# A recurrence of sixteen pairs of heads, regrouped: four pairs in lockstep instead of two staggered chains

## The chip, the cores and the metric

The kernel runs on one core of one Trainium2 chip, as one program. The metric is device time in microseconds of one launch; the time of a kernel is the median of its runs. The engines are named as in the profile: PE (matrix multiplication, with PEld its weight loads), DVE (vector), ACT (scalar), POOL (GpSimd), SP (here it issues nearly all DMAs).

## The reference, cut to what matters

A trunk of two layers over 512 tokens of width 2048. Layer 0 is a gated attention and is untouched. Layer 1 is RWKV-7 time mixing with 32 heads of 64:

```python
def step(S, inp):
    r_t, w_t, k_t, v_t, a_t, b_t = inp
    sa = jnp.einsum('bhvk,bhk->bhv', S, a_t)
    S = S * w_t[:, :, None, :] + sa[..., None] * b_t[:, :, None, :] \
        + v_t[..., None] * k_t[:, :, None, :]
    y_t = jnp.einsum('bhvk,bhk->bhv', S, r_t)
    return S, y_t
...
_, y = lax.scan(step, S0, xs)
...
y = (y - mean) * lax.rsqrt(var + LNX_EPS)
y = y * lnx_w.reshape(H, N).astype(f32) + lnx_b.reshape(H, N).astype(f32)
y = y + jnp.sum(rh * kh * r_k.astype(f32), axis=-1, keepdims=True) * vh
...
return (y * jax.nn.silu(z)) @ w_out
```

`r`, `k`, `v` and `z` are four projections of 2048 by 2048 of mixed inputs; decay `w`, `a` and a part of `v` come from small low-rank products.

## The kernel before, in words

Activations lie with features on the 128 partitions and the 512 tokens on the free axis, so a tile of 128 features is a pair of heads: 16 pairs, j = 0 to 15. Each projection is 16 tiles of 16 steps, and a step is three matmuls of 128x128 by 512 columns (`mm3`: high by high, low by high, high by low part of the float32 operands). On PE these are the rows `pj<-hi,whi`, `pj<-hi,wlo`, `pj<-lo,whi`; I call the three a triple. Their weights come by DMA (`raw<-in_wr`, `in_wv`, `in_wz`, `in_wo`), four triples to a load; ACT makes the high part (`whi`), DVE the low one (`wlo`).

**What sets the order.** Every engine issues in the order in which the code was written, and that order comes from a planner, `Flow`: side tasks are generators that yield planned delays, and `backbone` writes the projection triples and lets due tasks put their instructions between them. Its clock advances with the columns of the matmuls written. `HOP` is the planned length of a step of the recurrence. The layer-1 tiles run in the order r, v, z, output.

**The recurrence** is done by chunks of 64 tokens, eight per pair. What a chunk needs is made earlier by `keys` (tensors `atd`, `bkd` in DRAM), by `invert` and `inverse` (`qtd`), by `lora_up` (`ipd`), `recept` (`rTd`) and `values` (`vvd`, and transposed `vtd`), each stored for a pair with `sp.dma_start`.

`stage` (line 1454) loads a pair: `rt`, `bk` in four DMAs, `prk`, and for each half of four chunks `L`, `QP` (two DMAs for each head) and `SV`. Four halves may be staged ahead (`free["half"]`). `stage_half` makes the products of a half: for each chunk and head one `S<-L,bk` matmul of 128 columns, copied by ACT to `L` and `GP`, masked by POOL, then transposes `S<-ident,bk` copied to `tok`. At the end of a pair it makes a bonus term (`bv`, with two means matmuls `S<-mhi`, `S<-mlo`).

`chain` (line 1567) runs a pair's eight chunks, one after the other, in three steps per chunk. In each a few float32 matmuls of 64 columns, for the two heads, go to PE, and DVE takes the result:

- `x<-SV,L` and `y<-L,SV`; DVE copies `x` to `xs`, POOL scales the state for the next chunk (`SV<-SV,dec`);
- `x<-xs,QP`; DVE copies it to `SV`, over the state just read;
- `x<-SV,tok`; DVE adds it to the next chunk's `SV`; `y<-GP,SV` finishes the output. A last chunk has no `x<-SV,tok`.

`hop` waits for the planner's next multiple of `HOP`. Two pairs are active at a time, half a pair apart, so PE gets two pairs' matmuls of a step together. When a pair ends, `chain` normalizes it (`S<-mhi,centerr`, `S<-mhi,blkr`, scale and shift on DVE) and stores `ypd`; `gated` multiplies by the z projection.

SP's queue is one for all of these loads and stores and for the weights. A DMA that waits holds what stands behind it.

Of the kernel before, what the change touches and what calls it, by code (L numbers as in the profile page):

```python
# [17 lines left out]
P = 128  # L18
# [7 lines left out]
NCH = T // C  # L26
LW, LA_, LV = 96, 96, 64
# [102 lines left out]
def body(ctx, tc, a, out, dbg=None, stop=0):  # L130
# [81 lines left out]
    atd = dr.tile([KT, P, NCH, C], F, name="atd")  # L212
    bkd = dr.tile([KT, P, 2, NCH, C], F, name="bkd")
# [4 lines left out]
    ipd = dr.tile([KT, P, T], F, name="ipd")  # L218
    aad = dr.tile([KT, P, T], F, name="aad")
    svd = dr.tile([KT, P, T], F, name="svd")  # L220
    rTd = dr.tile([KT, P, T], F, name="rTd")
    vvd = dr.tile([KT, P, T], F, name="vvd")
    vtd = dr.tile([KT, T, P], F, name="vtd")
    ypd = dr.tile([KT, P, T], F, name="ypd")
# [806 lines left out]


# [22 lines left out]
    free = {"m": NHP, "eI": 1, "eN": 1, "bk": 1, "B": 1, "gab": 12, "qt": 5, "half": 4, "prk": 2, "sv": 1, "vf": 2}  # L1055
# [149 lines left out]
    def lora_up(q, j, n):  # L1205
# [20 lines left out]
        sp.dma_start((ipd, aad, svd)[n][j], t)  # L1226
# [5 lines left out]
    def values(j, o, e):  # L1232
# [16 lines left out]
        sp.dma_start(vvd[j], vv)  # L1249
# [9 lines left out]
        sp.dma_start(vtd[j].rearrange("(i p) c -> p i c", i=4), vt)  # L1259
# [22 lines left out]
    def keys(q, j):  # L1282
        ip = load(q, ipd[j], "ip", bufs=2)
# [42 lines left out]
        sp.dma_start(atd[j], at)  # L1326
        sp.dma_start(bkd[j], bk)
# [122 lines left out]
    QP, GP, staged = [], [], {}  # L1450

    HC = NCH // 2

    def stage(q, j):
        eI = q.tile([P, NCH, C + 1], F, tag="eI", name="eI", bufs=2)
        rt = load(q, rTd[j], "rt", bufs=2)
        bk = q.tile([P, NCH, 2, C], F, tag="bk", name="bk", bufs=2)
        yield 1
        for i in range(2):
            sp.dma_start(bk[0:64, :, i, :], bkd[j][0:64, i])  # L1460
            sp.dma_start(bk[64:128, :, i, :], bkd[j][64:128, 1 - i])
            yield 1
        dec = q.tile([P, NCH], F, tag="dec", name="dec", bufs=3)
        yield from take("prk")
        prk = q.tile([P, NCH, C], F, tag="prk", name="prk", bufs=2)
        sp.dma_start(prk, ipd[j].rearrange("p (c t) -> p c t", c=NCH))
        rv = c3(rt)
        for cc in range(2):
            yield from take("half")
            cs = slice(HC * cc, HC * cc + HC)  # L1470
            L, SV = ([q.tile([P, HC] + w, F, tag=f"{n}{h}", name=f"{n}{h}", bufs=4)
                      for h in range(2)] for n, w in (("L", [2, C]), ("SV", [C])))
            qp, gp = QP[(2 * j + cc) % 4], GP[(2 * j + cc) % 4]
            for h in range(2):
                s, t = HS[h], OS[h]
                sp.dma_start(L[h][s, :, 0, :], atd[j][s, cs])
                for p in range(2):
                    sp.dma_start(qp[h][s, p::2, :],
                                 qtd[j, 64 * p:64 * p + 64,
                                     4 * h + HC // 2 * cc:4 * h + HC // 2 * (cc + 1), :])  # L1480
                yield 0.5
            while j not in vd:
                yield 0.2
            for h in range(2):
                s, t = HS[h], OS[h]
                sp.dma_start(SV[h][t], vtd[j].rearrange("(c t) d -> t c d", c=NCH)[:, cs, s])
                if cc == 0:
                    pool.memset(SV[h][HS[h], 0, :], 0.0)
            fl.start(fl.t, stage_half(q, j, cc, L, SV, qp, gp, bk, eI, rv, dec, prk))
            yield 3  # L1490

    def stage_half(q, j, cc, L, SV, qp, gp, bk, eI, rv, dec, prk):
        cs = slice(HC * cc, HC * cc + HC)
        yield STW if j else 12
        if cc == 0:
            pool.memset(eI[:, :, 0:1], 1.0)
            act.activation(eI[:, :, 1:], prk, AF.Exp, scale=-EDEC)
            yield 2
            pool.tensor_copy(dec, eI[:, :, C])
        for h in range(2):  # L1500
            s = HS[h]
            dve.tensor_tensor(out=L[h][s, :, 1, :], in0=rv[s, cs], in1=eI[s, cs, 1:],
                              op=OP.mult)
            yield 0.6
            dve.scalar_tensor_tensor(out=prk[s, cs], in0=L[h][s, :, 1, :],
                                     scalar=vecs[s, V_RK, j:j + 1],
                                     in1=bk[s, cs, 1 - h, :], op0=OP.mult, op1=OP.mult)
            yield 0.6
        yield 0.7
        ns = yield from need2("S")  # L1510
        gs = [bank("S") for _ in ns]
        for c in range(HC):
            for h in range(2):
                s = HS[h]
                pe.matmul(gs[h][:, c * P:(c + 1) * P],
                          bk[s, HC * cc + c].rearrange("p a t -> p (a t)"),
                          L[h][s, c].rearrange("p a t -> p (a t)"), start=True, stop=True)
        yield 0.7
        for h in range(2):
            s, t = HS[h], OS[h]  # L1520
            g3 = gs[h].rearrange("p (c n) -> p c n", c=HC)
            act.activation(L[h][t].rearrange("p c a t -> p c (a t)"), g3[t], AF.Copy)
            act.activation(gp[h][s], g3[s, :, C:], AF.Copy)
            read("S", ns[h])
            pool.affine_select(out=L[h][t], in_=L[h][t], pattern=[[0, HC], [1, 2], [1, C]],
                               compare_op=OP.is_ge, fill=0.0, base=-1,
                               channel_multiplier=-1)
            pool.affine_select(out=gp[h][s], in_=gp[h][s], pattern=[[0, HC], [1, C]],
                               compare_op=OP.is_ge, fill=0.0, base=0,
                               channel_multiplier=-1)  # L1530
            yield 0.9
        pool.tensor_tensor(out=bk[:, cs], in0=bk[:, cs],
                           in1=eI[:, cs, C:C + 1].unsqueeze(2).broadcast_to([P, HC, 2, C]),
# [4 lines left out]
        for c in range(HC):  # L1538
            pe.transpose(tr[:, c * P:(c + 1) * P],
                         bk[:, HC * cc + c].rearrange("p a t -> p (a t)"), ident)  # L1540
        yield 0.5
        tok = q.tile([P, HC, 2, C], F, tag="tok", name="tok", bufs=4)
        act.activation(tok.rearrange("p c h t -> p (c h t)"), tr, AF.Copy)
        read("S", n)
        staged[j, cc] = L, SV, qp, gp, dec, tok
        if cc == 0:
            return
        vv = load(q, vvd[j], "vv", bufs=1)
        yield from take("B")
        bo, n = yield from means(q, blkr, prk.rearrange("p c t -> p (c t)"), "mh", "ml")  # L1550
        free["B"] += 1
        yield 0.7
# [5 lines left out]
        staged[j] = bv  # L1558

    active = set()  # L1560
# [6 lines left out]
    def chain(q, j):  # L1567
        active.add(j)
        y = bank("y")
        for c in range(NCH):  # L1570
            last = c == NCH - 1
            i, n = c % HC, (c + 1) % HC
            if i == 0:
                L, SV, qp, gp, dec, tok = staged.pop((j, c // HC))
                nSV = SV
# [254 lines left out]
```

## Time and profile before

| | us |
|---|---|
| median of 3 runs | 2463.61 (2460.46 to 2463.98) |
| the profiled execution's own time | 2465.95 |
| its span, first to last instruction | 2464.2 |
| mean granted clock of PE | 0.983 |
| first and last chain matmul `x<-SV,L` start | 1758.0, 2274.1 |
| last `y<-GP,SV` starts | 2278.6 |
| share of the chain that ended last: PE, of it pj | 72%, 56% |

All operations go through one helper, so every row of the profile has the line L88 (L90 in the changed program) and is told apart by its tiles, written out<-in. Times in windows and timelines are from the span's start. A float32 matmul of 64 columns, and one of 64 rows by 128 columns, leaves two records each: the 256 `x<-SV,L` of the program are 512 in the trace.

### The profile page before, as it was taken

The page shows a single profiled execution, that of the slowest core. Times are in us where ns is not written, and L with a number is a line of the kernel's source. Part 1 is how long each engine was busy: PE and PEld are TensorE (multiplying, and loading weights), DVE is VectorE, ACT ScalarE, POOL GpSimd, SP SyncE. Part 2 cuts the span into 40 slices and gives each one's busy share as a digit, 9 for nine tenths or more (in the row PEclk, how much of TensorE's full clock was granted, in tenths as well). Part 3 has the DMA queues.
Part 4 walks back from the last instruction along what each step waited for, and adds up shares of the span by engine and source line. Part 5 has one row for each costly group of instructions (what it writes and reads, how often), then busy time and mean ns, then how long its engine had stood idle before and what let it go on. Part 6 is the DMA issues. An engine that isn't in the chain of part 4 may idle for free.

```text
span 2464.2 us, 39831 instructions
## 1 busy us (share of the span) xinstructions
PE 2354.1 (96%) x13626; PEld 1811.6 (74%) x13626; DVE 1648.8 (67%) x3130; ACT 1259.0 (51%) x2301; POOL 709.2 (29%) x1154
## 2 busy tenths in 40 slices
PE   6998899999999999998999998989899999999999
PEld 4786677777777778886766776767677677777887
DVE  6977778787887544337796667763467867776322
ACT  3435656555555544226547777743334555555321
POOL 0002424434333100110240239830334444441000
PEclk8999999999999999999999999999899999999999
DMA  8865566666665264445657898867666755554443
GB/s 305 321 221 182 175 198 206 210 206 210 204 213 171 92 227 157 147 137 176 205 168 248 290 287 252 278 208 203 180 169 171 193 161 160 161 161 149 148 146 95
DMA packets 341563, 480.25 MB, mean 195 GB/s; under 512 B 146544, under 2 KB 156912, under 8 KB 337520
## 3 DMA queue, kind: packets, MB, share of 16 engines
q1 hardware_dynamic: 339696, 475.08, 61.5%
q0 software_dynamic: 1664, 2.63, 0.3%
q8 instruction: 108, 1.77, 0.3%
q14 instruction: 95, 0.78, 0.1%
HBM read 381.63 MB, written 95.95 MB: 194 GB/s over the span
## 4 chain that ended last, share of the span: by engine, by line
PE 72%; DVE 8%; DMA 6%; POOL 6%; ACT 4%; issue 3%; SPq 1%; DVEq 0%; ACTq 0%; POOLq 0%
PE pj L88 56%; PE S L88 6%; PE x L88 4%; POOL lane L88 3%; POOL lt L88 3%; PE tr L88 2%; PE pv L88 2%; DVE wlo L88 2%; DVE m L88 2%; PE ss L88 1%; PE y L88 1%; SPq L88 1%; DMA wm<-in_wmodT 1%; DVE wm L88 1%; ACT whi L88 1%
## 5 line engine op out<-in xcount | busy, mean ns | idle before, releaser
L88 PE MATMUL pj<-hi,whi 128*128 128x512 f32 x2416 | 997.9, 413 | 13.3 <-ACT hi L88 8.2
L88 PE MATMUL pj<-hi,wlo 128*128 128x512 f32 x2416 | 959.8, 397 | 6.1 <-DVE wlo L88 6.1
L88 PE MATMUL pj<-lo,whi 128*128 128x512 f32 x2416 | 960.6, 398 | 0.0
L88 DVE TENSOR_TENSOR wlo<-raw,whi 128x512 fp32r<-128x512 f32 (+2 forms) x628 | 479.7, 771 | 263.9 <-ACT whi L88 250.1
L88 ACT ACTIVATE whi<-raw 128x512 fp32r<-128x512 f32 (+2 forms) x628 | 394.5, 634 | 442.2 <-PE pj L88 246.6
L88 PEld LDWEIGHTS pj<-hi,whi 128*128 128x128 f32 x2416 | 459.7, 190 | 119.8 <-ACT hi L88 9.0
L88 PEld LDWEIGHTS pj<-lo,whi 128*128 128x128 f32 x2416 | 458.6, 190 | 108.2 <-DVE lo L88 0.2
L88 PEld LDWEIGHTS pj<-hi,wlo 128*128 128x128 f32 x2416 | 460.6, 191 | 96.3 <-DVE wlo L88 8.1
L88 POOL TENSOR_SCALAR SV<-SV,dec 64x64 f32<-64x64 f32 x224 | 95.7, 428 | 211.7 <-DVE SV L88 196.6
L88 DVE CUSTOM_DVE_ANT_0 wm<-wm,cb 128x1024 f32<-128x1024 f32 x128 | 156.3, 1221 | 0.3
L88 ACT ACTIVATE pr<-Sm,mx 128x128 f32<-128x128 f32 (+3 forms) x128 | 71.6, 559 | 88.9 <-POOL mx L88 88.8
L88 POOL TENSOR_SCALAR mx<-mx 128x1 f32<-128x1 f32 x128 | 65.7, 513 | 162.5 <-DVE mx L88 115.8
L88 POOL TENSOR_SCALAR pr<-pr,rc 128x128 f32<-128x128 f32 (+3 forms) x128 | 97.1, 758 | 28.8 <-DVE rc L88 20.5
L88 DVE COPY SV<-x 64x64 f32<-64x64 f32 x256 | 56.8, 222 | 63.6 <-PE x L88 56.5
L88 DVE CUSTOM_DVE_ANT_0 Sm<-S,cmask 128x128 f32<-128x128 f32 (+3 forms) x128 | 62.2, 486 | 37.2 <-PE S L88 36.6
L88 POOL TENSOR_TENSOR lt<-lane 128x30 f32<-128x30 f32 (+14 forms) x90 | 62.4, 693 | 55.2 <-DMA lane<-mld 48.3
L88 POOL TENSOR_TENSOR lane<-lane,lt 128x30 f32<-128x30 f32 (+14 forms) x90 | 67.8, 753 | 7.0
L88 DVE TENSOR_TENSOR SV<-SV,x 64x64 f32<-64x64 f32 x224 | 49.0, 219 | 25.1 <-PE x L88 19.4
L88 PE MATMUL S<-k,q 128*128 128x128 f32 (+7 forms) x256 | 62.4, 324 | 1.5 <-DMA k<-krow 1.5
L88 POOL TENSOR_TENSOR acc<-acc,sq 128x512 f32<-128x512 f32 x14 | 18.1, 1296 | 150.7 <-ACT sq L88 128.3
L88 PE MATMUL tr<-ident,pr 128*128 128x128 f32 x320 | 56.7, 275 | 4.5 <-ACT pT L88 1.7
L88 PEld LDWEIGHTS tr<-ident,pr 128*128 128x128 f32 x320 | 41.3, 140 | 25.1 <-ACT pT L88 7.9
(324 smaller groups left out, 3376.4 us busy)
## 6 DMA issues: line engine op xcount, KB each, us to landing
wm<-in_wmodT SPq DMA_DIRECT2D x132, 512.0 KB, 4.2
raw<-in_wz SPq DMA_DIRECT2D x128, 256.0 KB, 3.8
raw<-in_wo SPq DMA_DIRECT2D x128, 256.0 KB, 3.5
raw<-in_wv SPq DMA_DIRECT2D x124, 256.0 KB, 3.6
wm<-in_wmodT SPq DMA_DIRECT2D x30, 1024.0 KB, 6.8
raw<-in_wk SPq DMA_DIRECT2D x96, 256.0 KB, 3.7
raw<-in_wr SPq DMA_DIRECT2D x64, 256.0 KB, 4.9
raw<-in_wq SPq DMA_DIRECT2D x56, 256.0 KB, 3.5
```

The source lines that it names most:

```text
L88: self.last = f(*a, **k)
```

## The change

Pairs are taken in four groups of four (`NJ = 4`), and chunks in units of two (`UC = 2`; `NG = 4` groups, `NU = 4` units). One task, `recur`, runs 32 chunk steps of four pairs each, in place of two staggered `chain`s. A step now has eight matmuls of a kind in a row (four pairs, two heads); the DVE copies and adds of a head cover four pairs, 64x256, and the tok product has an `x` bank of its own. `HOP` goes from 2.0 to 3.9. Each chunk but a group's last has three steps with `x`, so there are 32 x 3 - 4 = 92 steps that have an `x` product.

`stage` loads a unit of two chunks of four pairs: `rt`, four `bk`, `prk`, then for each chunk and head one `L`, one `QP` and one `SV` load; four chunks may be staged ahead. It waits for the vectors of all four pairs. `products` makes one chunk's products, `bonus` and `normed` work on a unit; scale, shift and the bonus factor differ by pair and are now applied in four pieces. `gated` takes one of two tokens for its z tile. The DRAM tensors that staging reads are laid out by group and unit, so that their stores by pair are in pieces of 128 tokens (512 B); `bkd` and `vtd` are stored by two DMAs each, `vtd` in pieces of 64 features (256 B).

The core of the diff:

```diff
-    atd = dr.tile([KT, P, NCH, C], F, name="atd")
-    bkd = dr.tile([KT, P, 2, NCH, C], F, name="bkd")
+    atd = dr.tile([NG, P, NU, NJ, UC * C], F, name="atd")
+    bkd = dr.tile([NG, P, NU, 2, NJ, UC * C], F, name="bkd")
...
-    vtd = dr.tile([KT, T, P], F, name="vtd")
+    vtd = dr.tile([NG, T, 2, NJ, DH], F, name="vtd")
...
-        sp.dma_start(vtd[j].rearrange("(i p) c -> p i c", i=4), vt)
+        for h in range(2):
+            sp.dma_start(vtd[j // NJ].rearrange("(i p) h j d -> h j p i d", i=4)[h, j % NJ],
+                         vt[:, :, DH * h:DH * h + DH])
...
-        sp.dma_start(bkd[j], bk)
+        for i in range(2):
+            sp.dma_start(bkd[j // NJ][:, :, i, j % NJ], u3(bk[:, i].rearrange("p c t -> p (c t)")))
...
+        while any(NJ * g + i not in vd for i in range(NJ)):
+            yield 0.2
+        for c in range(UC):
+            yield from take("chunk")
...
+                sp.dma_start(L[h][s, :, 0, :], atd[g][s, u, :, c * C:c * C + C])
+                dve.tensor_copy(L[h][s, :, 1, :], rt[s, :, c])
+                sp.dma_start(qp[h][s], qtd[NJ * g:NJ * g + NJ, 64 * c:64 * c + 64,
+                                           4 * h + u, :].rearrange("j p t -> p j t"))
+                sp.dma_start(SV[h][t], vtd[g][(UC * u + c) * C:(UC * u + c + 1) * C, h])
...
+    def recur(q):
+        for m in range(NG * NCH):
...
+            for j in range(NJ):
+                for h in range(2):
+                    pe.matmul(x[HS[h], 0, j], L[h][:, j, 0, :], SV[h][:, j, :],
+                              start=True, stop=True, skip_group_check=True)
+            xs = q.tile([P, NJ, C], F, tag="xs", name="xs", bufs=2)
+            dve.tensor_copy(xs, x[:, 0])
...
             for h in range(2):
                 s = HS[h]
+                for j in range(0 if last else NJ):
+                    pool.tensor_scalar(nSV[h][s, j, :], SV[h][s, j, :], dec[s, j, c:c + 1],
                                        1.0, op0=OP.mult, op1=OP.mult)
             yield from hop()
+            for j in range(NJ):
+                for h in range(2):
+                    pe.matmul(x[HS[h], 1, j], qp[h][:, j, :], xs[:, j, :],
+                              start=True, stop=True, skip_group_check=True)
             for h in range(2):
-                dve.tensor_copy(SV[h][HS[h], i, :], x[HS[h], C:2 * C])
+                dve.tensor_copy(SV[h][HS[h]], x[HS[h], 1])
...
-    HOP = 2.0
+    HOP = 3.9
```

How the order moves. First PE, in the middle of the recurrence, before: the second step of a chunk (`x<-xs,QP`) of the two active pairs, among triples of a projection.

```order
L88 MATMUL pj<-hi,wlo 128x512
L88 MATMUL pj<-lo,whi 128x512
L88 MATMUL x<-xs,QP_17032 64x64
L88 MATMUL x<-xs,QP_17033 64x64
L88 MATMUL x<-xs,QP_17024 64x64
L88 MATMUL x<-xs,QP_17025 64x64
L88 MATMUL pj<-hi,whi 128x512
```

The same step in the changed program; each pair of rows is the two heads of one of the four pairs.

```order
L90 MATMUL pj<-lo,whi 128x512
L90 MATMUL x<-xs,QP_17042 64x64
L90 MATMUL x<-xs,QP_17043 64x64
L90 MATMUL x<-xs,QP_17042 64x64
L90 MATMUL x<-xs,QP_17043 64x64
L90 MATMUL x<-xs,QP_17042 64x64
L90 MATMUL x<-xs,QP_17043 64x64
L90 MATMUL x<-xs,QP_17042 64x64
L90 MATMUL x<-xs,QP_17043 64x64
L90 MATMUL pj<-hi,whi 128x512
```

A run of four has become a run of eight, and there are fewer of them; what is written between two triples without a projection matmul in between is one run.

Then SP, at the first staging, while the v projection's weights are loaded, before: the loads of pair 0's halves.

```order
L88 DMA L_17082<-atd 64x4x64
L88 DMA QP_17016<-qtd 64x2x64 x2
L88 DMA raw<-in_wv 128x512
L88 DMA L_17083<-atd 64x4x64
L88 DMA QP_17017<-qtd 64x2x64 x2
L88 DMA SV_17084<-vtd 64x4x64
L88 DMA SV_17085<-vtd 64x4x64
L88 DMA raw<-in_wv 128x512
```

In the changed program, the first chunk's loads, behind the store of pair 3's vectors (`vtd<-vt`).

```order
L90 DMA raw<-in_wv 128x512
L90 DMA vtd<-vt 128x4x64 x2
L90 DMA L_17198<-atd 64x4x64
L90 DMA QP_17034<-qtd 64x4x64
L90 DMA SV_17200<-vtd 64x256
L90 DMA L_17199<-atd 64x4x64
L90 DMA QP_17035<-qtd 64x4x64
L90 DMA SV_17201<-vtd 64x256
L90 DMA raw<-in_wv 128x512
```

The first chunk's six loads stand together, right behind the last store they need; fewer staging loads stand between the first weight loads, as they come later.

More of the change, by code (lines that the diff above doesn't have):

```diff
@@ L1464, in stage @@
         yield from take("prk")
[L1465 to L1473, printed above, removed]
+        prk = q.tile([P, NJ, UC, C], F, tag="prk", name="prk", bufs=2)
@@ L1477, in stage @@
[L1477 to L1488, printed above, removed]
@@ L1604, in chain @@
                 for h in range(2):
                     s = HS[h]
-                    dve.tensor_tensor(out=nSV[h][s, n, :], in0=nSV[h][s, n, :],
-                                      in1=x[s, 2 * C:3 * C], op=OP.add)
-            for h in range(2):
-                pe.matmul(y[HS[h], c * C:(c + 1) * C], SV[h][:, i, :], gp[h][:, i, :],
-                          start=False, stop=True, skip_group_check=True)
-            if i == HC - 1:
-                free["half"] += 1
-            if not last:
-                yield from hop()
@@ L1669, in gated @@
         yield 1
+        free["z"] += 1
         if j < KT - 2:
```

268 lines of the change are left out of this document (143 added, 125 removed).

## The prediction

> **What bounds the kernel now.** First the page's busy shares, then the stretch in which the recurrence runs, by windows (PE, PEld, DVE, ACT and POOL busy, granted clock, DMA share, GB/s).
>
> ```profile
> PE 2354.1 (96%) x13626; PEld 1811.6 (74%) x13626; DVE 1648.8 (67%) x3130; ACT 1259.0 (51%) x2301; POOL 709.2 (29%) x1154
> ```
> ```profile
> 1400.00:1500.00 100.00, 92.54 (x461) 70.83 (x461) 74.23 (x93) 77.02 (x139) 43.08 (x53) 0.99 0.90 289
> 1500.00:1600.00 100.00, 93.24 (x817) 72.15 (x813) 75.78 (x95) 74.23 (x144) 89.90 (x126) 0.98 0.87 268
> 1700.00:1800.00 100.00, 87.16 (x536) 65.70 (x535) 45.20 (x101) 29.28 (x53) 28.27 (x70) 0.93 0.70 186
> 1800.00:1900.00 100.00, 98.58 (x892) 72.17 (x891) 72.56 (x195) 44.30 (x83) 42.68 (x87) 1.00 0.62 171
> 1900.00:2000.00 100.00, 94.58 (x835) 69.23 (x833) 79.46 (x204) 53.77 (x97) 46.87 (x88) 0.98 0.66 181
> 2000.00:2100.00 100.00, 99.41 (x900) 72.76 (x900) 70.72 (x193) 57.63 (x96) 45.66 (x90) 1.00 0.58 158
> 2100.00:2200.00 100.00, 99.44 (x902) 72.40 (x903) 72.04 (x195) 61.14 (x98) 43.31 (x88) 1.00 0.59 162
> 2200.00:2300.00 100.00, 99.12 (x693) 73.11 (x694) 65.85 (x154) 54.59 (x90) 23.77 (x42) 1.00 0.47 151
> ```
>
> From 1800 to 2300 PE idles only 8.9 us (1.4 + 5.4 + 0.6 + 0.6 + 0.9). The recurrence is hidden beside the projections, and what sets the end is PE's own work. So a change counts here if it makes that work shorter or lets PE wait. The one weak place is 1700 to 1800: 12.8 us idle, and a mean clock of 0.93. The waits of PE over the recurrence, and the window around that place, say when:
>
> ```profile
> PE S L88 <- ACT vt L88: 5.9, 1, 5.9
> PE x L88 <- DVE SV L88: 4.5, 13, 0.9
> PE pj L88 <- ACT whi L88: 3.5, 1, 3.5
> ```
> ```profile
> 1723.00:1754.00 31.00, 18.16 (x75) 13.02 (x74) 13.61 (x25) 8.96 (x17) 8.79 (x15) 0.78 0.77 206
> ```
>
> All 12.8 us lie between 1723 and 1754 (31.00 less 18.16), just as staging begins, and the clock there averages 0.78. If it switches between full and half, it was at half for 0.44 of 31 us, 13.6 us, which costs at most another 6.8. The start of the recurrence is thus worth up to 19.6 us. Why ACT was late, from the timelines of ACT and SP:
>
> ```profile
> 1726.22 0.63 ACT L88 ACTIVATE whi<-raw 128x512 fp32r<-128x512 f32 x1 [6.22 <-DMA raw<-in_wv]
> ```
> ```profile
> 1719.41 1.26 SPq L88 DMA_DIRECT2D QP<-qtd  x2
> 1720.72 1.26 SPq L88 DMA_DIRECT2D SV<-vtd  x2
> ```
>
> Staging loads take SP about 0.63 us each, and weight loads (raw) stand behind them in the same queue.
>
> **PE's work: fewer runs.** The matmuls of recurrence and staging are the same in number and shape in both programs. What differs is how they are bunched. On PE they interrupt a stream of projection matmuls, and an interruption costs more than its matmuls. Two interruptions (a matmul of 64 columns leaves two records):
>
> ```profile
> 2039.76 0.40 PE L88 MATMUL pj<-lo,whi 128*128 128x512 f32 x1
> 2040.09 0.45 PE L88 MATMUL x<-xs,QP 128*64 128x64 f32 x8
> 2040.47 0.50 PE L88 MATMUL pj<-hi,whi 128*128 128x512 f32 x1
> 2040.80 0.39 PE L88 MATMUL pj<-hi,wlo 128*128 128x512 f32 x1
> 2041.03 0.39 PE L88 MATMUL pj<-lo,whi 128*128 128x512 f32 x1
> ...
> 2042.43 0.40 PE L88 MATMUL pj<-lo,whi 128*128 128x512 f32 x1
> 2042.76 0.34 PE L88 MATMUL x<-SV,tok 128*64 128x64 f32 x4
> 2042.92 0.29 PE L88 MATMUL y<-GP,SV 128*64 128x64 f32 x4
> 2043.04 0.29 PE L88 MATMUL x<-SV,tok 128*64 128x64 f32 x4
> 2043.15 0.29 PE L88 MATMUL y<-GP,SV 128*64 128x64 f32 x4
> 2043.37 0.50 PE L88 MATMUL pj<-hi,whi 128*128 128x512 f32 x1
> 2043.71 0.39 PE L88 MATMUL pj<-hi,wlo 128*128 128x512 f32 x1
> ```
>
> Undisturbed, pj starts are 0.23 apart (2040.80, 2041.03). Within a run, four records take 0.115 (2042.92 to 2043.15 is eight in 0.23), so 0.029 each. From the last pj before a run to the second pj after it there are two pj steps, 0.47, and the records. The first run: 1.04 - 0.47 - 8 x 0.029 = 0.34 us over. The second, twice as long: 1.28 - 0.47 - 16 x 0.029 = 0.35. So the extra hangs on the run and not on its length. A run of transposes alone, with the median of one such transpose:
>
> ```profile
> 1877.02 0.39 PE L88 MATMUL S<-mlo,centerr 128*128 128x512 f32 x1
> 1877.25 0.60 PE L88 MATMUL S<-ident,bk 128*128 128x128 f32 x4
> 1877.61 0.48 PE L88 MATMUL pj<-hi,whi 128*128 128x512 f32 x1
> 1877.93 0.39 PE L88 MATMUL pj<-hi,wlo 128*128 128x512 f32 x1
> ```
> ```profile
> L88 PE MATMUL S<-ident,bk x128: 270/273/421, 1757.5 to 2239.1; 128*128 128x128 f32 x128
> ```
>
> Four transposes are (0.60 - 0.27) / 3 = 0.11 apart, 0.44 in all; 0.91 - 0.47 - 0.44 leaves nothing. They are free of the extra. The means of 512 columns (S<-mlo) are of pj's kind, and I count them with pj.
>
> Counted in the two orders from the first staging product on, runs that hold chain matmuls or staging products fall from 217 to 102; staging products are part of 32 runs in both. 115 x 0.34 = 39 us less PE work. Bounds: 0 if the extra is not the run's, and 115 x 0.35 = 40.
>
> The Trainium skill, "TensorE: Matmul & The Clock Gate", section "Back-to-back issue gap", gives a steady gap of the columns over 2.4 GHz plus about 2.5 ns, with no term for a change of kind between neighbours; by it alone this term would be 0 and the sum 2455. The rows above disagree with it at both chain runs, so I go by the rows.
>
> **The start.** From the first load of a stage on, SP has 50 other DMAs to issue before its eighth weight load in the old order and 26 in the new, 53 and 36 before the tenth: the first stages are halves of two pairs before, two chunks of four pairs now. 24 fewer at 0.63 us is 15 us of SP's time, more than the 12.8 of PE's idling. Against it, the vectors of pairs 0 to 3 are all needed before the first chunk, and their last store and the first load of it stand close together in the new order; SP waits there with weight loads behind it. Later the new order is the denser one (120 against 100 before the 25th). I take half of the 19.6, -10; the ends are -19.6 (no stall left) and +10 (half as much again as before).
>
> **Other edits.** Rows of the operations that change shape, from the views of their tiles:
>
> ```profile
> L88 DVE COPY SV<-x x256: 205/223/230, 1760.8 to 2276.6; 64x64 f32<-64x64 f32 x128
> L88 DVE TENSOR_TENSOR SV<-SV,x x224: 202/220/227, 1763.0 to 2271.9; 64x64 f32<-64x64 f32 x112
> L88 DVE TENSOR_TENSOR L<-rt,eI x64: 407/422/789, 1730.3 to 2228.1; 64x256 f32<-64x256 f32 x64
> L88 POOL TENSOR_SCALAR SV<-SV,dec x224: 310/319/1996, 1730.0 to 2266.2; 64x64 f32<-64x64 f32 x112
> L88 SPq DMA_DIRECT2D bkd<-bk x16: 320/376/403, 1399.2 to 1594.0; - x16
> ```
>
> DVE's 256 copies and 224 adds of 64 columns become 64 and 56 of 256. No PSUM read of 64x256 is in the trace; from 0.22 (64 columns) to 0.42 (256 columns from SBUF) I take the latter: 256 x 0.223 + 224 x 0.22 = 106 us become 50. Splitting prk and the scale and shift by pair gives some of that back. DVE is 66 to 79% busy and hidden by PE, so 0; without the cover it would still be a gain. POOL keeps its 224 decays, but eight stand in a row, 8 x 0.32 = 2.6 us, ahead of the copy that overwrites what they read. In the order, three to five triples of pj, 2.1 to 3.5 us, and a run of 0.8 lie between: enough, though not by much; 0, bounded by the second rival. DMA issues: 64 fewer for QP, 16 more each for bkd and vtd. Stores of bkd come while DMA is 0.90 and 0.87 busy (1400 to 1600), now in pieces of 512 B: from 0 (PE's waits there are on DVE) to 16 x 0.38 = 6 us if each extra issue delays PE; +2, nearer the hidden end. Table loads fall by three, off the path.
>
> **Sum.** Against the profiled execution's own 2465.95 (span 2464.2): -39 - 10 + 2 = 2419. That execution was 2.3 over the median of the runs shown, 2463.61, so the forecast is 2416.
>
> **Rivals.**
> 1. *One chain, more waits.* Two independent chains become one; 92 steps each wait for DVE. For: PE already waited for DVE SV 13 times, 4.5 us, 0.35 each. Against: in the new order most steps stand three to six triples apart, at least 2.1 us, against two copies of 0.42 and one DVE operation ahead. At 0.35 for each step, 92 x 0.35 = 32: 2448.
> 2. *The stall of the start comes back with every group.* Four groups begin with loads for four pairs; if SP's staging holds weight loads back each time, PE loses 19.6 four times instead of once, +59, and -39 + 2 remain: 2485, slower. It decides where more than about four loads of 0.63 stand per weight load while a weight load lasts PE four triples (2.8 us) with no recurrence beside them. For: the later order is denser. Against: from the second group on each triple has recurrence work beside it, so weight loads are needed more rarely, and only four chunks may be staged ahead.
> 3. *The extra is not the run's.* It moves with the steps' matmuls instead: -10 + 2: 2455. The two run lengths speak against it.
> 4. *Short stores of the vectors.* vtd is written in pieces of 256 B instead of 512. If that doubles a landing of 5.3 us,
>
> ```profile
> vtd<-vt SPq DMA_DIRECT2D x3, 256.0 KB, 5.3
> ```
>
> SP waits 5.3 longer ahead of the first chunk, the gain of the start is gone too: 2465.95 - 39 + 5.3 + 2 - 2.3 = 2432. The Trainium skill, "DMA: Bandwidth & Descriptors", section "Specifications", puts line rate at 512 B and up, with read-modify-write below. No run here shows it yet.
>
> That the bunching does not come about is excluded by the order: eight matmuls of a step stand in a row.
>
> **Chances.** Forecast 0.70, its own range 2396 (all of the start and the 8.9 us of idling won) to 2436 (the start +10). Rival 1: 0.14; 2: 0.07; 3: 0.05; 4: 0.04. The range reaches to rival 1, 2396 to 2450, and leaves out 2, 3 and a tail of the forecast. A measurement of this kernel can tell about 0.2%, 5 us, from no change. Slower takes rival 2 and a little of 1, 0.08; within 0.2% are the edges of 1 and 3, 0.04; faster is the rest, 0.88.
>
> **What would show it.** Right: PE busy from the first product to the end of the recurrence about 39 us shorter at unchanged matmul counts; the extra of 0.34 at runs of 16 and 32 records alike; less idling than 12.8 us where staging starts. Wrong: an extra that grows with the run (3); many short waits on DVE SV or xs in PE's list (1); waits on ACT whi at each group's start and a clock under 1.00 there (2); a late vtd with SP's load of SV behind it (4). I am wrong if PE's work falls and its idling rises by as much.

## The result and the profile after

The changed kernel took 2427.65 us (median of 4 runs, 2426.07 to 2435.13), the kernel before 2463.8 in the same comparison (4 runs, 2460.46 to 2468.75). The ratio is 0.9858, with a 95% interval of 0.9831 to 0.9884: faster by 1.4%. The forecast of 2416 was 11.65 us too low, inside its range. The two profiled executions took 2465.95 and 2426.40.

The busy shares of the changed kernel, from its page. PE has lost 42 us of work at the same 13626 instructions, and DVE 42:

```profile
PE 2312.1 (95%) x13626; PEld 1806.3 (74%) x13626; DVE 1607.0 (66%) x2850; ACT 1254.5 (52%) x2298; POOL 701.4 (29%) x1114
```

To compare equal work I count the triples of projection matmuls, which stand in the same order in both programs; a triple is placed by the start of its `pj<-hi,whi`. Triple 1344 is where the stage of the keys begins, 1600 is behind it, staging begins at about 1728, and the recurrence has ended by 2176. The windows between these triples, first of the kernel before (span of the window, then busy us of PE, PEld, DVE, ACT and POOL, the granted clock, the DMA share, GB/s); the rows are triples 1344 to 1600, 1600 to 2176, and inside the latter 1728 to 1792 and 1792 to 1920:

```profile
1360.20:1604.30 244.10, 226.73 (x1513) 175.12 (x1512) 173.96 (x217) 183.10 (x338) 148.29 (x204) 0.99 0.87 277
1604.30:2293.00 688.70, 659.39 (x5602) 489.22 (x5601) 459.81 (x1155) 340.58 (x593) 247.17 (x480) 0.98 0.62 174
1720.40:1809.30 88.90, 76.06 (x530) 56.04 (x529) 43.24 (x106) 28.16 (x52) 27.77 (x56) 0.92 0.67 179
1809.30:1987.80 178.50, 171.66 (x1531) 125.52 (x1529) 139.87 (x359) 89.45 (x163) 76.24 (x150) 0.99 0.65 177
```

The same work in the changed kernel:

```profile
1351.60:1604.00 252.40, 230.87 (x1513) 177.14 (x1512) 171.67 (x217) 183.10 (x338) 146.28 (x203) 0.97 0.91 268
1604.00:2252.60 648.60, 616.62 (x5602) 485.26 (x5602) 422.01 (x877) 337.12 (x591) 242.00 (x441) 0.98 0.66 185
1718.70:1805.70 87.00, 79.11 (x707) 61.71 (x707) 55.10 (x112) 36.83 (x68) 35.70 (x66) 0.96 0.71 187
1805.70:1987.70 182.00, 167.54 (x1654) 130.91 (x1652) 136.48 (x280) 93.64 (x173) 87.83 (x155) 0.97 0.73 193
```

From triple 1600 to 2176 PE did the same 5602 records in 42.8 us less busy time. Its idle time there went from 29.3 (688.70 less 659.39) to 32.0. The stage of the keys took 8.3 longer; half of that is idling (17.4 to 21.5), and half is the same 1513 records taking 4.1 longer at a granted clock of 0.97 instead of 0.99. Up to triple 1344 the changed kernel was 8.6 ahead (1360.2 less 1351.6), and behind triple 2176 it lost 0.8. In sum: -8.6 + 8.3 - 40.1 + 0.8 = -39.6, the difference of the profiled executions (39.55).

What PE waited for from 1690 to 2290, changed kernel:

```profile
PE S L90 <- ACT vt L90: 6.6, 2, 3.8
PE S L90 <- DVE mlo L90: 4.2, 4, 1.6
PE S L90 <- DVE vf L90: 3.1, 1, 3.1
...
PE x L90 <- DVE xs L90: 1.0, 1, 1.0
```

The chain itself hardly waits. What waits is work on the S banks: staging products, transposes and means that stand in PE's order before the engines ahead of them are done.

### The profile page after: what moved, and what is told of

Its sections match the earlier page's. It is cut to its first block, busy times and chain, and to the rows that moved or that the text cites. A ratio compares the mean times of both kernels' runs of the same rounds, so it can differ in the third digit from the quotient of the medians.

```text
span 2424.7 us, 39355 instructions
## 1 busy us (share of the span) xinstructions
PE 2312.1 (95%) x13626; PEld 1806.3 (74%) x13626; DVE 1607.0 (66%) x2850; ACT 1254.5 (52%) x2298; POOL 701.4 (29%) x1114
## 5 line engine op out<-in xcount | busy, mean ns | idle before, releaser
L90 PE MATMUL pj<-hi,whi 128*128 128x512 f32 x2416 | 986.6, 408 | 11.9 <-ACT hi L90 8.2
L90 DVE TENSOR_TENSOR wlo<-raw,whi 128x512 fp32r<-128x512 f32 (+2 forms) x628 | 474.4, 762 | 281.7 <-ACT whi L90 279.3
L90 POOL TENSOR_SCALAR SV<-SV,dec 64x64 f32<-64x64 f32 x224 | 98.3, 461 | 113.5 <-DVE SV L90 71.5
L90 POOL TENSOR_TENSOR bk<-bk,eI 128x512 f32<-128x512 f32 x32 | 36.4, 1137 | 105.9 <-PE S L90 90.1
L90 DVE SCALAR_TENSOR_TENSOR hp<-pj,gate,hp 128x512 f32<-128x512 f32 x16 | 12.0, 751 | 68.8 <-PE pj L90 68.8
## 6 DMA issues: line engine op xcount, KB each, us to landing
raw<-in_wz SPq DMA_DIRECT2D x128, 256.0 KB, 3.8
raw<-in_wo SPq DMA_DIRECT2D x128, 256.0 KB, 3.5
raw<-in_wv SPq DMA_DIRECT2D x124, 256.0 KB, 3.8
raw<-in_wk SPq DMA_DIRECT2D x96, 256.0 KB, 3.6
raw<-in_wr SPq DMA_DIRECT2D x64, 256.0 KB, 4.6
raw<-in_wq SPq DMA_DIRECT2D x56, 256.0 KB, 3.5
```

The lines of the kernel that those rows point to most:

```text
L90: self.last = f(*a, **k)
```

## The experiments

Twelve further runs were made, one of them the changed kernel again. The theory of the prediction was an extra of 0.34 us for each run of chain matmuls. After comparing the two traces a second one stood beside it: the extra is paid at each change of the tile shape that PE's rows name (`128*128`, `128*64` or `64*128`), about 0.17 each, twice for a plain run. (The shape is the pair that stands in each row ahead of the operands' sizes; 128*128 is the full one.) The rival to both was an extra that goes with the matmuls.

**What the extra belongs to: e1_split.** Each step is broken after two of its four pairs:

```diff
                     pe.matmul(x[HS[h], 0, j], L[h][:, j, 0, :], SV[h][:, j, :],
                               start=True, stop=True, skip_group_check=True)
+                if j == 1:
+                    yield 0.95
```

(and the same in the other two steps)

> The new kernel with each of the three matmul steps of a chunk broken after two of its four pairs, so that projection triples come between the halves. Nothing else is changed. Runs that hold chain matmuls or staging products rise from 102 to 158; changes of the tile shape on PE (128*128 for projections, means and transposes, 128*64 for the chain, 64*128 for the staging products) rise from 230 to 389. Theory of the prediction (0.34 us per run): +56 x 0.345 = +19 us of PE busy time, about 2447. Second theory, formed from the rows of both traces (runs of chain matmuls cost 0.35, runs of staging products alone 0.38, runs with both 0.54, runs of transposes 0): the cost is 0.17 us for each change of tile shape: +159 x 0.172 = +27 us, about 2455, with runs of 0.35 for chain matmuls and about 0.7 where products stand between chain matmuls. Rival (the extra belongs to the steps' matmuls, whose number is unchanged): 0, 2428.

Measured: 2475.35 us, ratio to before 1.0058 (1.0045 to 1.0071), slower than before and above all three forecasts. From triple 1728 to 2176, split kernel first, changed kernel second:

```profile
1725.90:2298.70 572.80, 538.57 (x4625) 405.31 (x4624) 358.16 (x738) 285.75 (x495) 216.86 (x397) 0.98 0.59 166
```
```profile
1718.70:2252.60 533.90, 509.31 (x4626) 399.88 (x4626) 355.40 (x742) 289.83 (x499) 217.01 (x397) 0.98 0.65 179
```

PE's busy time rose by 29.3, nearer to the 27 of the shape than to the 19 of the run; the matmuls are the same, so the rival is out. Between the two theories this sum alone is weak: the later kernels with the matmul order of the changed one are busy for 503.4 (e4) to 516.9 (e10) there, and for 529.5 in e3, where the granted clock is 0.92. The rest of the loss in this stretch, 9.6, is idling, which no theory had named: the later halves come so late that the next step waits for its copy.

```profile
PE x L90 <- DVE xs L90: 14.6, 9, 3.0
```

The rows of single runs tell the two theories apart. In the changed kernel, a chain run with products behind it:

```profile
2009.25 0.40 PE L90 MATMUL pj<-lo,whi 128*128 128x512 f32 x1
2009.58 0.69 PE L90 MATMUL x<-SV,L 128*64 128x64 f32 x16
2010.09 0.64 PE L90 MATMUL y<-L,SV 128*64 128x64 f32 x16
2010.66 1.16 PE L90 MATMUL S<-L,bk 64*128 64x128 f32 x16
2011.75 0.50 PE L90 MATMUL pj<-hi,whi 128*128 128x512 f32 x1
2012.09 0.39 PE L90 MATMUL pj<-hi,wlo 128*128 128x512 f32 x1
```

In the split kernel, with the products between the halves of a step:

```profile
2026.71 0.40 PE L90 MATMUL pj<-lo,whi 128*128 128x512 f32 x1
2027.04 0.45 PE L90 MATMUL x<-SV,tok 128*64 128x64 f32 x8
2027.42 1.16 PE L90 MATMUL S<-L,bk 64*128 64x128 f32 x16
2028.51 0.45 PE L90 MATMUL x<-SV,tok 128*64 128x64 f32 x8
2028.80 0.64 PE L90 MATMUL y<-GP,SV 128*64 128x64 f32 x16
2029.36 0.50 PE L90 MATMUL pj<-hi,whi 128*128 128x512 f32 x1
2029.70 0.39 PE L90 MATMUL pj<-hi,wlo 128*128 128x512 f32 x1
```

Both are one run of 48 records of the same kinds, 32 chain and 16 products. From the last pj ahead to the second pj behind, the first takes 2.84 and has three changes of shape; the second takes 2.99 and has four. One change more costs 0.15, in one and the same run.

What a change does stands in the rows of PEld, PE's weight loads. Of the first run, the loads at its first and its last change:

```profile
2009.58 0.55 PEld L90 LDWEIGHTS x<-SV,L 128*64 128x64 f32 x16 [0.36 <-issue]
...
2011.75 0.19 PEld L90 LDWEIGHTS pj<-hi,whi 128*128 128x128 f32 x1
```

Each starts with its own matmul (2009.58 and 2011.75 above) and not ahead of it. At each of the 230 changes of shape from 1700 to 2300 the load starts at most 0.03 us ahead of its matmul; where one pj follows another, the load starts 0.23 us ahead. So at a change the weight load waits for its matmul's turn, instead of running ahead beside the matmuls before it.

**The shape alone: e2_qp_full.** The middle step is written in PE's full shape; the two halves of QP stand side by side in one tile, and those that were zero stay zero.

```diff
-                for h in range(2):
-                    pe.matmul(x[HS[h], 1, j], qp[h][:, j, :], xs[:, j, :],
-                              start=True, stop=True, skip_group_check=True)
+                pe.matmul(x[:, 1, j], qp[:, j].rearrange("p h t -> p (h t)"), xs[:, j, :],
+                          start=True, stop=True, skip_group_check=True)
```

> The new kernel with the middle step (x from xs and QP) written as one matmul of full 128*128 tile shape for each pair, instead of two of 128*64: both heads' halves of QP stand side by side in one tile, with the zeros they already had. Four matmuls of about 0.107 instead of eight of 0.058: -1 us over 32 steps. The runs on PE stay as they are (102 against 101 that hold chain matmuls or products); the changes of tile shape fall from 230 to 174. If the extra is the run's (the prediction's theory): -1 us, 2427, and 0.35 stays at the runs of this step alone. If the extra is paid for each change of tile shape: -56 x 0.172 - 1 = -11 us, about 2417, and runs of this step alone show no extra, as runs of transposes do.

Measured: 2433.99, ratio 0.9886 (0.9871 to 0.9901): not faster than the changed kernel. The row of such a run shows why:

```profile
2024.36 0.39 PE L90 MATMUL pj<-lo,whi 128*128 128x512 f32 x1
2024.59 1.00 PE L90 MATMUL x<-xs,QP 128*128 128x64 f32 x8
2025.39 0.48 PE L90 MATMUL pj<-hi,whi 128*128 128x512 f32 x1
2025.71 0.39 PE L90 MATMUL pj<-hi,wlo 128*128 128x512 f32 x1
```
```profile
2024.36 1.09 PEld L90 LDWEIGHTS x<-xs,QP 128*128 128x128 f32 x8
```

1.35 from pj to second pj, less two pj steps of 0.47, leaves 0.88 for eight records, 0.11 each. That is the spacing of the transposes, which also use the full shape, so nothing is left for an extra, and its first weight load starts 0.23 ahead of its matmul (2024.36, 2024.59). The run does the work of a step, interrupts the projections as before, and pays nothing: the extra is the change of shape and not the run. My price of the matmuls was wrong, though. I had 0.107 for each of four; it is 0.22 (two records of 0.11, the pace of the weight loads too, whose columns are now 128 instead of 64), 0.88 for a step against 16 x 0.029 = 0.46. Two matmuls of half the width, one for each head, thus cost half of one full one. 56 changes fewer save 56 x 0.17 = 9.5, and 32 x 0.42 = 13.4 is lost: +3.9; PE's busy time from triple 1728 to 2176 is 512.34, 3.0 over the changed kernel's, which agrees but is within the spread given above.

**The stage of the keys: e3_keys_layout and e8_keys_one_store.** In e3, atd, bkd and ipd are laid out by pair again:

```diff
-        sp.dma_start(of(atd, j), u3(at.rearrange("p c t -> p (c t)")))
-        for i in range(2):
-            sp.dma_start(bkd[j // NJ][:, :, i, j % NJ], u3(bk[:, i].rearrange("p c t -> p (c t)")))
+        sp.dma_start(atd[j], at)
+        sp.dma_start(bkd[j], bk)
...
+                for j in range(NJ):
+                    sp.dma_start(bk[HS[h], j, :, i, :],
+                                 bkd[NJ * g + j, HS[h], i ^ h, UC * u:UC * u + UC, :])
```

(ipd, and the loads of prk and L, likewise)

> The new kernel with the three side tensors that the stage of the keys writes (atd, bkd, ipd) laid out by pair as in the kernel before, so their stores are whole rows again and one store for bkd instead of two. The loads of a stage gather from four pairs, bk with 16 loads instead of 4 (96 more issues on SP in the recurrence). From projection triple 1344 to 1600 the new kernel took 252.4 us and the old one 244.1. If the layout of these stores makes the 8 us: this stretch takes about 244 to 246, triple 1600 starts about 7 us earlier. Rival (small waits on VectorE and clock slots that fall differently by chance, the layout has no part): the stretch stays at 250 to 253. The end may be later by what 96 loads of 0.6 us on SP hold up, so the verdict is read at triple 1600 and not at the end.

Measured up to triple 1600, as planned, 247.3 against 252.4:

```profile
1356.50:1603.80 247.30, 228.07 (x1513) 175.79 (x1512) 172.86 (x217) 183.51 (x338) 146.83 (x204) 0.99 0.88 273
```

Two later kernels with these layouts gave 249.4 and 246.4, and eight with the new layouts 250.9 to 256.0, mean 253.1. The means differ by 5.4. The packets from 1400 to 1600 show what the DMAs do; before, changed, and e3:

```profile
DMA packets 50908, 55.74 MB, mean 279 GB/s; under 512 B 27970, under 2 KB 27970, under 8 KB 50887
```
```profile
DMA packets 77375, 52.75 MB, mean 264 GB/s; under 512 B 26904, under 2 KB 62744, under 8 KB 77354
```
```profile
DMA packets 54861, 54.46 MB, mean 272 GB/s; under 512 B 27823, under 2 KB 33967, under 8 KB 54840
```

The end of e3 was the surprise: 2513.99, ratio 1.0217 (1.0204 to 1.0230), 86 us over the changed kernel. Its loads of bk are 256 instead of 64, 16 in each of 16 stages, so SP has 192 more to issue, not the 96 of the expectation, and they stand ahead of weights. One place, SP's queue first, then ACT:

```profile
1835.99 3.20 SPq L90 DMA_DIRECT2D bk<-bkd  x5
...
1839.93 0.45 SPq L90 DMA_DIRECT2D raw<-in_wv  x1
```
```profile
1844.29 0.63 ACT L90 ACTIVATE whi<-raw 128x512 fp32r<-128x512 f32 x1 [8.41 <-DMA raw<-in_wv]
```

In e8 the two stores of bkd of a pair are one, by another order inside the tile; the pieces stay 512 B:

```diff
-        for i in range(2):
-            sp.dma_start(bkd[j // NJ][:, :, i, j % NJ], u3(bk[:, i].rearrange("p c t -> p (c t)")))
+        sp.dma_start(bkd[j // NJ].rearrange("p u i j t -> p (u i) j t")[:, :, j % NJ],
+                     bt.rearrange("p u i t -> p (u i) t"))
```

> The new kernel with the two stores of bkd of each pair written as one, by another order inside the tile; the pieces in DRAM stay 512 B. The old layout gave back 5 of the 8 us that the stage of the keys had grown by (247.3 from triple 1344 to 1600, against 250.9 to 254.7 in four runs of the new one and 244.1 before). If the number of issues makes them (16 more of 0.38): this stretch takes 246 to 249. If the short pieces do (packets in 1400 to 1600 rose from 50908 to 77375): it stays at 250 to 255, and the time at 2427.

Measured: the stretch took 250.7, the time was 2429.76 (ratio 0.9856, 0.9841 to 0.9870). That is just below the spread of the new layout and no gain in the end: the number of issues is not shown to matter, and the pieces remain the likely cause. Whether they cost at the DMA engines or on SP isn't separated: summed over SP's rows from triple 1344 to 1600, its issuing took 149.6 us before, 179.4 in the changed kernel, 152.3 in e3 and still 182.4 in e8.

**SP's queue: e4_pool_loads, e5_pool_all, e6_prk_first, e9_keys_bk_pool, e10_keys_pool_all.** Where the changed kernel's start still stalls, SP, ACT and PE read:

```profile
1725.03 0.52 SPq L90 DMA_DIRECT2D raw<-in_wv  x1
1725.60 0.59 SPq L90 DMA_DIRECT2D L<-atd  x1
1726.23 0.61 SPq L90 DMA_DIRECT2D QP<-qtd  x1
1726.89 0.61 SPq L90 DMA_DIRECT2D SV<-vtd  x1
```
```profile
1728.96 0.63 ACT L90 ACTIVATE whi<-raw 128x512 fp32r<-128x512 f32 x1 [2.48 <-DMA raw<-in_wv]
1729.49 0.58 ACT L90 ACTIVATE vt<-S 128x512 f32<-128x512 f32 x1
```
```profile
1730.12 1.52 PE L90 MATMUL S<-L,bk 64*128 64x128 f32 x14 [3.77 <-ACT vt L90]
```

Staging loads stand between the weight loads; ACT waits for weights; the eviction of vt stands behind that split; the products wait for its bank. In e4 the loads of the first four chunks are POOL's:

```diff
-                sp.dma_start(L[h][s, :, 0, :], atd[g][s, u, :, c * C:c * C + C])
+                ld = pool if m < 4 else sp
+                ld.dma_start(L[h][s, :, 0, :], atd[g][s, u, :, c * C:c * C + C])
```

(QP and SV likewise)

> The new kernel with the loads of L, QP and SV of the first four chunks (24 loads) issued by POOL instead of SP. In the new kernel PE idles 6.8 us between 1729 and 1745 and two clock slots there are at half: its staging products wait for an eviction of vt on ACT, which stands behind a weight split that waits for weights, whose load stood behind six of these loads on SP. If SP's issue order makes this stall: the idling falls to about 1 us and the slots are gone, -7 to -10 us, about 2419. Rival (the transfers themselves are the limit, or the loads arrive later from POOL): the stall stays or moves, 2426 to 2430.

Measured: 2423.76, ratio 0.9845 (0.9830 to 0.9861). Triples 1728 to 1792 of e4:

```profile
1723.20:1804.00 80.80, 75.51 (x708) 59.31 (x707) 54.63 (x109) 37.19 (x69) 41.97 (x82) 1.00 0.74 203
```

80.8 against 87.0, with the clock at 1.00 instead of 0.96 and 5.3 us idle instead of 7.9 (about 1 had been expected of the stall). The wait for vt at 1730 is gone, here and in e5, e6 and e12. So SP's order made a good part of this stall. From 1600 to 2176 e4 took 639.2 against 648.6. The profiled executions differ by 5.2 only, because this one of e4 was 4.3 behind at triple 1600 (1608.3 against 1604.0), and by its interval alone e4 can't be told from the changed kernel.

In e5 all 32 chunks load through POOL (the condition is dropped).

> The new kernel with the loads of L, QP and SV of all 32 chunks (192 loads) issued by POOL instead of SP; with the first four chunks alone it took 2423.76. If SP's issue order also makes the later stalls (PE idles 5.8 us between 1956 and 1964 there, where ACT waits 2.7 for prk and 1.2 for a weight load, both late from SP): 2415 to 2420. Rival: POOL issues a load in about 0.6 us, 115 us for all, in front of the decays and the masks; waits of PE on POOL's products (bk, SV, GP) appear, 2424 to 2440.

Measured: 2419.78, ratio 0.9819 (0.9803 to 0.9834), as expected: faster than both kernels, with an interval below that of the changed kernel's second measurement (e11, 0.9845 to 0.9895) and all but below that of its first (0.9831 to 0.9884). From triple 1792 to 1920 it took 175.9 against 182.0.

In e6, on top of e4, the load of prk stands ahead of those of bk:

```diff
         sp.dma_start(rt.rearrange("p j c t -> p j (c t)"), rTd[g][:, u])
+        yield from take("prk")
+        prk = q.tile([P, NJ, UC, C], F, tag="prk", name="prk", bufs=2)
+        sp.dma_start(prk.rearrange("p j c t -> p j (c t)"), ipd[g][:, u])
```

> As the kernel with the loads of the first four chunks on POOL (2423.76), and in each stage prk is loaded right behind rt, ahead of the four loads of bk. ACT waits there for prk (2.7 us at 1956) with the eviction of vt and the splits behind it. If that order on SP makes the stall: PE's idling between 1956 and 1964 falls from 5.8 to about 2 us and the two half clock slots there go, -3 to -6 us, 2418 to 2421. Rival (the wait moves to bk or to the weights): 2422 to 2425.

Measured: 2422.31, ratio 0.9831 (0.9813 to 0.9848), no difference to e4 that can be told. The stall at triple 1905 became longer: PE waited 5.3 for vt there instead of 3.3. A miss.

In e9 the 16 loads of bk in each stage of the layout by pair (256 in all, not the 128 of the expectation) are POOL's:

```diff
                 for j in range(NJ):
-                    sp.dma_start(bk[HS[h], j, :, i, :],
+                    pool.dma_start(bk[HS[h], j, :, i, :],
```

> As the kernel with the layouts of atd, bkd and ipd by pair (2513.99, 86 over the new kernel), with its 16 loads of bk in each stage issued by POOL instead of SP; the same loads of the same pieces, 128 in all. If the 86 us came from SP, where 96 more loads stand ahead of weights and of the loads of the next stage: they go, 2420 to 2435. If the short transfers themselves made them: 2480 to 2514. In between, if POOL's 77 us of issuing (128 of 0.6) stands ahead of the decays. The stage of the keys should again take about 247 from triple 1344 to 1600.

Measured: 2430.18, ratio 0.9871 (0.9849 to 0.9892). The same transfers from another queue, and 84 of the 86 us are gone. So e3 was slow by SP's queue and not by the transfers.

e10 adds all of e5's loads to e9; that makes 448 issues on POOL, 271 us of it, not the 320 and 192 of the expectation.

> The kernel before with the loads of L, QP and SV of all chunks on POOL as well (2419.78 with the grouped layouts). If both gains add (5 us in the stage of the keys, 8 from SP's queue): about 2415. Rival (320 issues of 0.6 on POOL, 192 us beside 225 of its own work, hold up the masks and decays that PE waits for): 2425 or more.

Measured: 2469.71, ratio 1.0032 (1.0019 to 1.0046). The gains don't add; POOL is now the queue in which something stands behind something, as the waits of PE on it in e9 and in e10 show:

```profile
PE S L90 <- POOL bk L90: 13.3, 4, 5.0
```
```profile
PE S L90 <- POOL bk L90: 54.1, 14, 10.7
```

e12_two_by_pair tries what costs no more loads: e5, with atd and ipd by pair and bkd in groups.

> The new kernel with the loads of L, QP and SV on POOL (2419.78 with that alone), and with atd and ipd laid out by pair, bkd left in groups: their stores are whole rows again, and no load of a stage is split into more. The layouts by pair of all three made the stretch from triple 1344 to 1600 5.4 us shorter (246.4 to 249.4 in three runs, against 250.9 to 256.0 in eight with the new layouts). If each of the three has its part: 249 to 251 in that stretch, 2416 to 2418 in all. Rival (bkd's stores, the largest, make it alone): 252 to 254 and 2420.

Measured: 2419.95, ratio 0.9831 (0.9815 to 0.9846), and 252.4 in the stage of the keys: no gain over e5, and by the numbers the rival's case. Whether bkd makes the 5.4 alone isn't settled, since 249 to 251 and 252.4 are close to what executions differ by.

**POOL's length: e7_decay_one.** The eight decays of a step become two broadcast operations:

```diff
-                for j in range(0 if last else NJ):
-                    pool.tensor_scalar(nSV[h][s, j, :], SV[h][s, j, :], dec[s, j, c:c + 1],
-                                       1.0, op0=OP.mult, op1=OP.mult)
+                if not last:
+                    pool.tensor_tensor(out=nSV[h][s], in0=SV[h][s],
+                                       in1=dec[s, :, c:c + 1].broadcast_to([64, NJ, C]),
+                                       op=OP.mult)
```

> The new kernel with the eight decays of a step (POOL, 64x64, 0.46 us mean, 224 in all) written as two operations of 64x256 with a broadcast factor; by the row of bk times eI (128x512, 1.13) an operation of 64x256 should take about 0.6, so POOL loses some 65 us of work. If POOL's length costs PE time, by its waits (POOL SV 2.4 us) or by holding up VectorE (four operations that take 1.1 us alone took 3.1 beside POOL's, and PE then waited 3.1 for vf): -3 to -5 us, about 2423. If POOL is off the path, as the prediction had it: 2427 to 2428.

Measured: 2433.85, ratio 0.9882 (0.9865 to 0.9898). The decays fell from 98.3 us (224 of 0.46) to 41.1 (56 of 0.74), PE's waits for them (`PE S <- POOL SV`) from 2.4 us to 0.7, and the recurrence from triple 1600 to 2176 took 649.1, as without it (648.6). POOL's decays are off the path.

**The changed kernel again: e11_after_again.**

> The new kernel unchanged, on the chip of these runs: 2424 to 2432, and a second profile of it. What differs between its two profiles (the stage of the keys, the stretch up to triple 1152, the waits in the recurrence) is chance of an execution and not of the change.

Measured: 2429.58, ratio 0.9870 (0.9845 to 0.9895). Its second profile took 256.0 in the stage of the keys (252.4 in the first) and 648.2 from triple 1600 to 2176 (648.6). The recurrence repeats to 0.4 us; the stage of the keys does not.

## Why the prediction was right, and where it failed

**What bounds the kernel: right.** PE's work set the end before and sets it now. The 42.8 us off its busy time from triple 1600 to 2176 are the gain. That DVE's 42 us less of work are worth nothing beside them was not tested; PE's waits on DVE came to 7.9 us over the recurrence before and to 9.0 now.

**Fewer runs, -39: right in size (42.8), wrong in its unit.** "The extra hangs on the run and not on its length" was half true: not on the length, but not on the run either. A plain run changes the tile shape twice, so 0.34 a run and 0.17 a change can't be told apart there; the prediction looked at plain runs and at transposes, and the free transposes were the hint that it counted and did not follow up. That the wrong unit gave the right size is luck of this change, in which both counts fall by about half; where they part, as in e1, it gives 19 for a measured 29.3. Changes of shape fall from 468 to 230 in the two orders, and 42.8 / 238 is 0.18; in e1 159 more cost 29.3, again 0.18. The weight load that no longer runs ahead is what PEld's rows show of it. The Trainium skill, "TensorEngine Tiling (Array Packing)", section "Key Properties", says that a change of the tiling mode, unlike one of the tile, drains TensorE. The runs here agree that such a change costs time, 0.15 to 0.18 us each; the prediction had cited another page of the Trainium skill, which has no such term, and missed this one.

**The start, -10: the step that failed.** Part of the stall at the start did go: from triple 1728 to 1792 PE idles 7.9 instead of 12.8, at a clock of 0.96 instead of 0.92. By the prediction's own reckoning of the clock this is 4.9 and 3.6 us, 8.5 together, near the 10. But from 1792 to 1920 it idles 14.5 instead of 6.8, at 0.97 instead of 0.99, which takes all of that back. The prediction named the reason ("later the new order is the denser one") and set no price on it. The sum for the whole recurrence is +2.7 idle instead of -10. That these stalls are SP's order is shown for the start by e4, and for part of the later ones by e5. Two remain in all kernels with the grouped layouts and the steps of the changed kernel, at triples 1844 and 1905; e6 did not remove the second. The first is PE's one wait of 3.1 for vf, which the last section follows to VectorE beside POOL; it isn't SP's. What would remove them was not found.

**Stores of the keys, +2: mis-sized.** The stage took 8.3 more in the profiles. e3, e9 and e10 put 5.4 on the layouts; the bound of 6 held for that, but the value taken, near the hidden end, did not. That the bound held is luck too: it priced 16 more issues at the old 0.376, and the new stores take longer each, 22.8 us for 32 against 5.9 for 16.

```profile
L90 SPq DMA_DIRECT2D bkd<-bk x32: 582/637/1649, 1390.7 to 1593.9; - x32
```

PE's waits there are on DVE in name, but ACT, whose splits DVE needs, waits for later weight loads: its idling ahead of the splits (`whi`) in that stage rose from 27.9 to 35.8 us, and was 31.5 in e3. This path from the stores to PE is read from the rows and not tested by itself. The other 3 are within what executions of this stage differ by (250.9 to 256.0 for the same layouts).

**What the forecast did not have: 8.6 us up to triple 1344.** 5.8 of them lie ahead of triple 1152, where nothing was changed. The profiles of the changed kernel and of the twelve, alike up to there, reach it between 1076.7 and 1082.5; before needed 1083.9, in its one profile. I take this as chance, which made the profiled difference look nearer to the forecast than its steps were. With it the terms close: against the forecast's 2419 for a profiled execution, -3.8 (runs), +12.7 (idling), +6.3 (keys), -8.6 (chance) and +0.8 (the rest) give 2426.4; it took 2426.40. Without the two parts that I call chance, -42.8 + 2.7 + 5.4 + 0.8 = -33.9, between the differences of the medians, 36.2 here and 32.5 in e11. The low end of the range is 2397.5 by the two terms that it names, not 2396; nothing hangs on it.

**Other edits, 0: right.** DVE's copies and adds of 256 columns took 0.42 each, as taken. Cutting POOL's decays by more than half gained nothing (e7), and waits on DVE's copies and adds came to 1.7 us in all.

**The rivals.** 1 (one chain, more waits) did not come, but e1 shows that it is near: steps that end later wait 14.6 us for their copies. 2 (stall at every group) did not come at its price: the groups begin just behind triples 1748, 1830, 1916 and 2007, and from 1920 to 2176 PE idles 2.2 us in all. Its price came in e3, where more loads stand on SP: PE idles 81.1 us from triple 1728 to 2176, spread over the stages, and the time is 2513.99, slower than before. The changed kernel has a mild form of it, the 7.7 us more of idling from triple 1792 to 1920, though not all of that is SP's. 3 is excluded by e1 and e2. 4: the stores of vtd in short pieces, each of half the size, land no later, 3.5 us against 3.4 before, in the rows from 1690 to 2000 (those from 1690 to 1725, ahead of the first chunk, 3.3 against 5.2):

```profile
vtd<-vt SPq DMA_DIRECT2D x30, 128.0 KB, 3.5
```
```profile
vtd<-vt SPq DMA_DIRECT2D x15, 256.0 KB, 3.4
```

## What to carry to other kernels

When small matmuls interrupt a stream of large ones, count the changes of the tile shape in PE's rows and not the interruptions, and put matmuls of one shape together. A layout in DRAM is chosen by how many loads it puts on the queue that also brings the weights: the change of order gave 40 us, and the same order with 192 more loads on that queue lost more than twice as much. Price the later, denser part of a queue as well as the place where the stall stood before.

## What the runs showed of the hardware

A change of PE's tile shape costs 0.15 to 0.18 us, and the weight load behind it starts with its matmul instead of up to 0.23 us ahead. At the full shape a 64-column f32 matmul takes 0.22, while two of half width, one for each head, take 0.12 together: four records of 0.029.

A load issued by POOL holds POOL for about 0.60 us (192 loads took 116 us in e5), during which its other work stands behind; e10 shows the limit.

VectorE is slower beside POOL. In e4 the same four operations of VectorE took 3.06 beside POOL's and 1.13 with POOL idle; first VectorE's rows, then POOL's at the first place:

```profile
1869.62 3.06 DVE L90 SCALAR_TENSOR_TENSOR dc<-dc,vecs,bv 128x128 f32<-128x128 f32 x4
...
1961.52 1.13 DVE L90 SCALAR_TENSOR_TENSOR dc<-dc,vecs,bv 128x128 f32<-128x128 f32 x4
```
```profile
1869.62 1.05 POOL L90 TENSOR_TENSOR bk<-bk,eI 128x512 f32<-128x512 f32 x1
1870.75 0.66 POOL L90 TENSOR_SCALAR_AFFINE_SELECT L<-L 64x512 f32<-64x512 f32 x1
```

PE then waited 2.99 us for vf, which stood behind them on VectorE; this is the stall at triple 1844. The Trainium skill, "SBUF — State Buffer", section "Who interferes with whom", has an exclusive lock between the two engines when VectorE has two inputs in SBUF; these rows agree. A kernel that keeps the two apart there was not tried.
